# The low half of w_up's weights by an accumulating transfer: a decoder layer in split float32 on one core

## The chip, the core and the metric

The kernel runs on one core of a Trainium2 chip. The metric is the device time of one execution in microseconds (us). The kernel before takes 1471.77 us, the median of three runs (1471.39 to 1471.92).

## What is computed

One layer of a decoder over 256 tokens of 2048 channels, in float32: attention and a gated short convolution side by side, merged by gates and added to the residual r; then a wide MLP; then a gate with a per-layer input. The part that the change touches is the MLP, cut from the reference:

```python
D_MODEL = 2048
SEQ = 256
D_FF = 4 * D_MODEL
...
        r = r + merged @ w_o[i]
        h = rms_norm(r, g_mlp[i])
        r = r + jnp.square(jax.nn.relu(h @ w_up[i])) @ w_down[i]
        h = rms_norm(r, g_ple[i])
        r = r + jax.nn.sigmoid(h @ w_ple_gate[i]) * (p[i] @ w_ple_proj[i])
```

## The kernel before

TensorE multiplies in float32r, which keeps fewer bits than float32. So each operand is split into a high part (the value rounded to float32r) and a low part (value minus high), and each product is made of three: high by high, high by low, low by high. All weights come from HBM as float32 and are split on the core; activations are split when they are made.

A *unit* is 128x2048 weights, 1 MiB, loaded by one transfer that SP issues into one of three `raw` buffers. `load_unit` (L117) splits it in two halves of 128x1024: for each half ScalarE makes `w_hi` (L88) and VectorE `w_lo` (L89). The pool `wp` has 7 buffers of half a unit each for `hi` and for `lo`, so the half that is seventh after another takes its buffers, once TensorE has read them. `load_rows` (L128) does the same for w_down, in pieces of 128x512.

The MLP is a loop over q = 0 to 3. In each, 16 units of w_up give 16 sums `ps_up` (`cols` and `mm`, L168 to L184): per unit 16 blocks k, the first 8 in the first half and the others in the second, each with one matmul of the high weights on both parts of x (512 columns) and one of the low weights on the high part (256 columns). ScalarE and VectorE then take each sum out of its bank (L188, L189), apply relu and the row factor `row1` (L440), square it (L441) and split it (L88, L89). Then 16 units of w_down follow (L154 to L156, `ps_dn`).

`row1` comes from `rstd_mlp`: eight small matmuls after the first w_up unit (L207), a scaling on VectorE (L82), a power on GpSimd (L83), two diagonals on VectorE (L215), and a matmul after the second unit (L217).

Every engine runs its instructions in its own order, which the framework's scheduler sets from the order of the program and the buffers; semaphores hold an instruction until its inputs are there and its buffer is free.

Of the kernel before, what the change touches and what calls it, by code (L numbers as in the profile page):

```python
# [8 lines left out]
F32 = mybir.dt.float32  # L9
F32R = mybir.dt.float32r  # L10
AF = mybir.ActivationFunctionType
ALU = mybir.AluOpType
# [3 lines left out]
P = 128  # L16
# [8 lines left out]
HALF = UNIT // 2  # L25
# [10 lines left out]
def hybrid_block_kernel(ctx: ExitStack, tc: tile.TileContext, ins: dict, out: bass.AP):  # L36
# [9 lines left out]
    nc = tc.nc  # L46

    const = ctx.enter_context(tc.tile_pool(name="const", bufs=1))
    wp = ctx.enter_context(tc.tile_pool(name="wp", bufs=7))
# [5 lines left out]
    def slot(shape, dtype, name):  # L55
        return bp.tile(shape, dtype, tag="slot", name=name)

    def bank(name):
        return acc.tile([P, CW], F32, tag="acc", name=name)
# [25 lines left out]
    def split(hi, lo, src, gain=None):  # L85

        if gain is None:
            nc.scalar.activation(hi, src, AF.Copy)  # L88
            nc.vector.tensor_sub(lo, src, hi.bitcast(F32))  # L89
        else:  # L90
            nc.scalar.activation(hi, src, AF.Copy, scale=gain)
            nc.vector.scalar_tensor_tensor(lo, src, gain, hi.bitcast(F32), op0=ALU.mult, op1=ALU.subtract)

    def xsplit(xs, k, src, gain=None):

        x = slot([P, 2, S], F32R, "x")
        split(x[:, 0, :], x[:, 1, :], src, gain)
        xs[k] = x
# [4 lines left out]
    def run_pending(n):  # L103
        for _ in range(min(n, len(pending))):
            pending.pop(0)()


    def split_half(raw, step=HALF, between=None):
        hi = wp.tile([P, HALF], F32R, tag="hi", name="w_hi")
        lo = wp.tile([P, HALF], F32R, tag="lo", name="w_lo")  # L110
        for i in range(0, HALF, step):
            if between:
                between(i // step)
            split(hi[:, i:i + step], lo[:, i:i + step], raw[:, i:i + step])
        return hi, lo

    def load_unit(w):  # L117

        raw = wp.tile([P, UNIT], F32, tag="raw", name="raw", bufs=3)
        nc.sync.dma_start(raw, w)  # L120
        return [split_half(raw[:, h * HALF:(h + 1) * HALF]) for h in range(2)]

    def load_half(w):
        raw = wp.tile([P, HALF], F32, tag="raw", name="raw", bufs=3)
# [18 lines left out]
    def rows(units, xs, name, pops=1):  # L143

        nu = len(units)
        ps = [bank(f"ps_{name}_{t}") for t in range(NT)]
        for u, load in enumerate(units):
            wt = load()
            for j in range(KU):
                k = KU * u + j  # L150
                hi, lo = (p[:, (j % 2) * CW:(j % 2 + 1) * CW] for p in wt[j // 2])
                for t in range(NT):
                    xh, xl = (xs[k][:, i, t * P:(t + 1) * P] for i in range(2))
                    nc.tensor.matmul(ps[t], xh, hi, start=k == 0, stop=False)  # L154
                    nc.tensor.matmul(ps[t], xh, lo, start=False, stop=False)  # L155
                    nc.tensor.matmul(ps[t], xl, hi, start=False, stop=k == KU * nu - 1)  # L156
            run_pending(pops)
        return ps

    def qkv(c, load=load_unit):  # L160
        return [lambda u=u: load(ins["w_qkv"][c, u]) for u in range(4)]

    def tiles(wname, n, us=range(4)):

        w = ins[wname]
        return [lambda u=u: load_rows(w[n:n + 4, :, u * CW:(u + 1) * CW]) for u in us]

    def mm(ps, wt, i, x, first, last):  # L168

        wh, wl = (p[:, (i % 8) * P:(i % 8 + 1) * P] for p in wt[i // 8])  # L170
        both = x.rearrange("p a s -> p (a s)")
        if not last:
            nc.tensor.matmul(ps, wh, both, start=first, stop=False)  # L173
        nc.tensor.matmul(ps[:, S:], wl, x[:, 0, :], start=False, stop=False)  # L174
        if last:
            nc.tensor.matmul(ps, wh, both, start=False, stop=True)  # L176

    def cols(wt, xs, name, at=0, nk=16, flush=None):

        ps = bank(f"ps_{name}")  # L180
        for k in range(nk):
            if k == flush:
                run_pending(len(pending))
            mm(ps, wt, at + k, xs[k], k == 0, k == nk - 1)  # L184
        return ps

    def total(dst, ps):
        nc.scalar.activation(dst, ps[:, S:], AF.Copy)  # L188
        nc.vector.tensor_add(dst, ps[:, :S], dst)  # L189

    def temp(name):
        return sm.tile([P, S], F32, tag="temp", name=name, bufs=8)
# [10 lines left out]
    def rstd_columns(ss, name):  # L203
        ps = trp.tile([P, NT], F32, tag="tr", name=f"ps_ss_{name}")
        for t in range(NT):
            for i in range(2):
                nc.tensor.matmul(ps[:, t:t + 1], ss[:, i, t * P:(t + 1) * P], ones[:, 0:1], start=i == 0, stop=i == 1)  # L207
        rstd = const.tile([P, NT], F32, name=f"rstd_{name}")
        rsqrt_mean(rstd, ps, D, NT)
        return rstd  # L210

    def rstd_rows(rstd, name):
        diag = slot([P, NT, P], F32, f"diag_{name}")
        for t in range(NT):
            nc.vector.tensor_scalar_mul(diag[:, t, :], ident, rstd[:, t:t + 1])  # L215
        ps = trp.tile([P, S], F32, tag="tr", name=f"ps_rstd_{name}")
        nc.tensor.matmul(ps, ones, diag.rearrange("p t s -> p (t s)"), start=True, stop=True)  # L217
        row = const.tile([P, S], F32, name=f"rstd_row_{name}")
        nc.scalar.activation(row, ps, AF.Copy)
        return row  # L220
# [124 lines left out]
    for j in range(8):  # L345
        cc, cx, cb = temp("cc"), temp("cx"), temp("cb")
        for i, dst in ((1, cc), (2, cx), (0, cb)):
            total(dst, cols(load_unit(w_in[8 * i + j]), xT, f"conv{i}_{j}"))
            nc.vector.tensor_mul(dst, dst, row0)
            run_pending(1)  # L350
        u = sm.tile([P, S + 2], F32, tag="u", name=f"u_{j}")
        nc.gpsimd.memset(u[:, 0:2], 0.0)
        nc.vector.tensor_mul(u[:, 2:], cc, cx)
        y = temp("y")
        nc.scalar.activation(y, u[:, 2:], AF.Copy, scale=col(W_CONV + 16 + j))
        nc.vector.scalar_tensor_tensor(y, u[:, 1:S + 1], col(W_CONV + 8 + j), y, op0=ALU.mult, op1=ALU.add)
        nc.vector.scalar_tensor_tensor(y, u[:, 0:S], col(W_CONV + j), y, op0=ALU.mult, op1=ALU.add)
        nc.vector.tensor_mul(y, y, cb)
        xsplit(convT, j, y)


    def transposed(n, src, done):

        ps = trp.tile([P, 2, S], F32, tag="tr", name=f"tr_{n}")
        for i in range(2):
            o = (n + i) % 4 * P
            for t in range(NT):
                nc.tensor.transpose(ps[:, i, t * P:(t + 1) * P], src[t][:, o:o + P], ident)
        done(n, ps)
# [36 lines left out]
    hT = {}  # L406
    ss1 = slot([P, 2, S], F32, "ss1")
    for n in range(16):
        add_to_r(n, cols(load_unit(ins["w_o"][n]), mT, f"o_{n}", flush=12))
        xsplit(hT, n, r[n // 2][:, n % 2, :], col(G_MLP + n))  # L410
        if n % 2 == 1:
            square_sum(ss1, n // 2, r[n // 2])
# [14 lines left out]
    for q in range(4):  # L427
        uT = {}
        ready = []
        for n in range(16):  # L430
            ready.append(cols(load_unit(ins["w_up"][16 * q + n]), hT, f"up_{q}_{n}"))
            if q == 0 and n == 0:
                rstd1 = rstd_columns(ss1, "mlp")
                continue
            if q == 0 and n == 1:
                row1 = rstd_rows(rstd1, "mlp")
            for ps in ready:
                a = temp("a")
                total(a, ps)
                nc.vector.scalar_tensor_tensor(a, a, 0.0, row1, op0=ALU.max, op1=ALU.mult)  # L440
                nc.scalar.activation(a, a, AF.Square)  # L441
                xsplit(uT, len(uT), a)
            ready = []
        for c in range(4):
            ps = rows(tiles("w_down", 16 * q + 4 * c), uT, f"dn_{q}_{c}")
            for t in range(NT):
                if q == 0:
                    d[c, t] = slot([P, CW], F32, f"d_{c}_{t}")
                    nc.scalar.activation(d[c, t], ps[t], AF.Copy)
                else:  # L450
                    nc.vector.tensor_add(d[c, t], ps[t], d[c, t])
            if q == 3:
                for n in (4 * c, 4 * c + 2):
                    pending.append(lambda n=n, m=(d[c, 0], d[c, 1]): transposed(n, m, end_r))
# [23 lines left out]
    ready = []  # L478
    for n in range(16):
# [22 lines left out]
        ready = []  # L502
# [55 lines left out]
```

## Time and profile before

| what | value |
|---|---|
| median of three runs | 1471.77 us |
| the profiled execution's own time | 1472.05 us |
| its span, first to last instruction | 1470.1 us |
| TensorE matmul (PE) busy | 1459.7 us, 99% |
| VectorE (DVE) busy | 895.6 us, 61% |
| ScalarE (ACT) busy | 757.8 us, 52% |
| GpSimd (POOL) busy | 11.2 us, 1% |
| DMA engines, mean rate | 189 GB/s |

The span is the profiled execution between its first and last instruction; its own time also counts what lies around it. Busy times of engines overlap, so they don't add up to the span. In views of the trace, L12 is line 12 of the kernel, PEld is TensorE's weight load, SPq is the queue of transfers that SP issues.

### The profile page before, as it was taken

How to read it: one execution, taken by the hardware profiler on the slowest of the kernel's cores; microseconds unless marked ns; L12 is line 12 of the kernel's file. 1: busy time of each engine (PE TensorE's matmuls, PEld its weight loads, DVE VectorE, ACT ScalarE, POOL GpSimd, SP SyncE). 2: the span in 40 equal slices, each digit the busy share in tenths (PEclk: the TensorE clock that was granted, in tenths of full speed). 3: DMA queues.
4: the chain of work that ended last, by engine and by line, in shares of the span. 5: the costliest groups of instructions: out<-in, count | busy, mean ns of one | idle time of the engine just before them, and what ended most of it. 6: DMA issues, size and time to landing. Idle time of an engine off the chain costs nothing.

```text
span 1470.1 us, 18933 instructions
## 1 busy us (share of the span) xinstructions
PE 1459.7 (99%) x7384; PEld 1237.6 (84%) x7384; DVE 895.6 (61%) x1360; ACT 757.8 (52%) x1287; POOL 11.2 (1%) x27
## 2 busy tenths in 40 slices
PE   8999999999999999999999999999999999999998
PEld 6888888888888888888888888888888888888887
DVE  7555676756464547666654566555665466666775
ACT  7655555544445444445544455445554455545543
POOL 0100000000000000000000000000000000000000
PEclk9999999999999999999999999999999999999999
DMA  8644445555555565555555555555555555555551
GB/s 315 228 173 172 172 173 174 180 191 200 186 186 200 183 248 191 180 182 191 182 190 200 187 185 190 185 198 195 178 195 186 191 200 174 200 179 189 184 203 55
DMA packets 87305, 278.35 MB, mean 189 GB/s; under 512 B 5040, under 2 KB 7344, under 8 KB 69296
## 3 DMA queue, kind: packets, MB, share of 16 engines
q1 hardware_dynamic: 87072, 277.11, 54.5%
q8 instruction: 58, 0.95, 0.3%
q14 instruction: 31, 0.25, 0.0%
q10 hardware_dynamic: 144, 0.04, 0.0%
HBM read 275.03 MB, written 2.10 MB: 189 GB/s over the span
## 4 chain that ended last, share of the span: by engine, by line
PE 99%; DMA 0%; DVE 0%; ACT 0%; issue 0%
PE ps_up L173 15%; PE ps_up L174 8%; PE ps_dn L156 8%; PE ps_dn L154 8%; PE ps_dn L155 8%; PE ps_conv L173 6%; PE ps_g L156 4%; PE ps_g L154 4%; PE ps_g L155 4%; PE ps_o L173 4%; PE ps_pg L173 4%; PE ps_conv L174 3%; PE ps_o L174 2%; PE ps_pg L174 2%; PE ps_y L156 2%; PE ps_y L154 2%
## 5 line engine op out<-in xcount | busy, mean ns | idle before, releaser
L89 DVE TENSOR_TENSOR w_lo<-raw,w_hi 128x512 fp32r<-128x512 f32 (+1 forms) x748 | 647.8, 892 | 412.1 <-ACT w_hi L88 407.1
L88 ACT ACTIVATE w_hi<-raw 128x512 fp32r<-128x512 f32 (+1 forms) x748 | 568.6, 789 | 474.1 <-PE ps_dn L156 173.9
L173 PE MATMUL ps_up<-x,w_hi 128*128 128x512 f32 x960 | 341.7, 399 | 0.0
L174 PE MATMUL ps_up<-x,w_lo 128*128 128x256 f32 x1024 | 277.1, 281 | 0.0
L173 PEld LDWEIGHTS ps_up<-x,w_hi 128*128 128x128 f32 x960 | 180.4, 188 | 41.6
L154 PE MATMUL ps_dn<-w_hi,x 128*128 128x512 f32 x512 | 199.8, 390 | 0.0
L156 PE MATMUL ps_dn<-w_hi,x 128*128 128x512 f32 x512 | 199.3, 389 | 0.0
L155 PE MATMUL ps_dn<-w_lo,x 128*128 128x512 f32 x512 | 199.2, 389 | 0.0
L174 PEld LDWEIGHTS ps_up<-x,w_lo 128*128 128x128 f32 x1024 | 193.2, 189 | 6.3
L173 PE MATMUL ps_conv<-x,w_hi 128*128 128x512 f32 x360 | 129.5, 402 | 0.0
L156 PEld LDWEIGHTS ps_dn<-w_hi,x 128*128 128x128 f32 x512 | 96.1, 188 | 20.2
L155 PEld LDWEIGHTS ps_dn<-w_lo,x 128*128 128x128 f32 x512 | 96.1, 188 | 20.0
L154 PEld LDWEIGHTS ps_dn<-w_hi,x 128*128 128x128 f32 x512 | 96.1, 188 | 19.4
L174 PE MATMUL ps_conv<-x,w_lo 128*128 128x256 f32 x384 | 103.5, 280 | 0.0
L154 PE MATMUL ps_g<-w_hi,x 128*128 128x512 f32 x256 | 99.9, 390 | 0.0
L156 PE MATMUL ps_g<-w_hi,x 128*128 128x512 f32 x256 | 99.6, 389 | 0.0
L155 PE MATMUL ps_g<-w_lo,x 128*128 128x512 f32 x256 | 99.6, 389 | 0.0
L173 PE MATMUL ps_pg<-x,w_hi 128*128 128x512 f32 x240 | 85.8, 399 | 0.0
L188 ACT ACTIVATE a<-ps_up 128x256 f32<-128x256 f32 x64 | 24.6, 384 | 118.7 <-PE ps_up L176 118.7
L173 PE MATMUL ps_o<-x,w_hi 128*128 128x512 f32 x240 | 85.6, 399 | 0.0
L173 PEld LDWEIGHTS ps_conv<-x,w_hi 128*128 128x128 f32 x360 | 67.6, 188 | 15.2
L174 PEld LDWEIGHTS ps_conv<-x,w_lo 128*128 128x128 f32 x384 | 72.5, 189 | 1.4
(184 smaller groups left out, 1686.0 us busy)
## 6 DMA issues: line engine op xcount, KB each, us to landing
raw<-in_w_up_dram SPq DMA_DIRECT2D x64, 1024.0 KB, 4.9
raw<-in_w_down_dram SPq DMA_DIRECT2D x64, 1024.0 KB, 5.1
raw<-in_w_in_dram SPq DMA_DIRECT2D x56, 1024.0 KB, 5.0
raw<-in_w_qkv_dram SPq DMA_DIRECT2D x20, 1024.0 KB, 4.9
raw<-in_w_branch_dram SPq DMA_DIRECT2D x16, 1024.0 KB, 5.1
raw<-in_w_o_dram SPq DMA_DIRECT2D x16, 1024.0 KB, 4.9
raw<-in_w_ple_gate_dram SPq DMA_DIRECT2D x16, 1024.0 KB, 5.1
raw<-in_w_qkv_dram SPq DMA_DIRECT2D x16, 256.0 KB, 5.8
```

The source lines that it names most:

```text
L88: nc.scalar.activation(hi, src, AF.Copy)
L89: nc.vector.tensor_sub(lo, src, hi.bitcast(F32))
L154: nc.tensor.matmul(ps[t], xh, hi, start=k == 0, stop=False)
L155: nc.tensor.matmul(ps[t], xh, lo, start=False, stop=False)
L156: nc.tensor.matmul(ps[t], xl, hi, start=False, stop=k == KU * nu - 1)
L173: nc.tensor.matmul(ps, wh, both, start=first, stop=False)
L174: nc.tensor.matmul(ps[:, S:], wl, x[:, 0, :], start=False, stop=False)
L188: nc.scalar.activation(dst, ps[:, S:], AF.Copy)
```

## The change

In w_up alone, the second half of each unit is split in another way. ScalarE makes the high part as before, then writes minus high into the low buffer, and a transfer issued by GpSimd adds the raw half onto it in place. VectorE's subtraction of that half is gone. The first half, and all other weights, are split as before. There are 64 such halves (4 times 16).

```diff
+    def split_half_dma(raw):
+
+        hi = wp.tile([P, HALF], F32R, tag="hi", name="w_hi")
+        lo = wp.tile([P, HALF], F32R, tag="lo", name="w_lo")
+        nc.scalar.activation(hi, raw, AF.Copy)
+        nc.scalar.activation(lo, hi.bitcast(F32), AF.Copy, scale=-1.0)
+        nc.gpsimd.dma_start(lo, raw, accum_op=ALU.add)
+        return hi, lo
+
-    def load_unit(w):
+    def load_unit(w, by_dma=False):
 
         raw = wp.tile([P, UNIT], F32, tag="raw", name="raw", bufs=3)
         nc.sync.dma_start(raw, w)
-        return [split_half(raw[:, h * HALF:(h + 1) * HALF]) for h in range(2)]
+        return [(split_half_dma if by_dma and h else split_half)(raw[:, h * HALF:(h + 1) * HALF]) for h in range(2)]
...
-            ready.append(cols(load_unit(ins["w_up"][16 * q + n]), hT, f"up_{q}_{n}"))
+            ready.append(cols(load_unit(ins["w_up"][16 * q + n], by_dma=True), hT, f"up_{q}_{n}"))
```

The order of TensorE's and of SP's instructions is the same in both kernels (only line numbers differ, by 9 after the new function). On ScalarE, in the middle of the first w_up phase, one beat stands so before (the sum of unit 4 is taken out, and the weights of a unit further on are split):

```order
L188 ACTIVATE a_5701<-ps_up_0_4_5668 128x256
L88 ACTIVATE w_hi_5864<-raw_5862 128x1024
L441 ACTIVATE a_5701<-a_5701 128x256
L88 ACTIVATE x_5706<-a_5701 128x256
L88 ACTIVATE w_hi_5868<-raw_5862 128x1024
L188 ACTIVATE a_5752<-ps_up_0_5_5719 128x256
```

and so with the change:

```order
L197 ACTIVATE a_5706<-ps_up_0_4_5673 128x256
L88 ACTIVATE w_hi_5872<-raw_5870 128x1024
L450 ACTIVATE a_5706<-a_5706 128x256
L88 ACTIVATE x_5711<-a_5706 128x256
L121 ACTIVATE w_hi_5876<-raw_5870 128x1024
L122 ACTIVATE w_lo_5877<-w_hi_5876 128x1024
L197 ACTIVATE a_5758<-ps_up_0_5_5725 128x256
```

Minus high (L122) stands right behind the high part of the second half, ahead of the next sum's evacuation. On GpSimd, which had nothing to do between the convolution's memsets and the two powers, the queue now holds 64 transfers (L123), the first four of them ahead of the power for `rstd_mlp`:

```order
L361 MEMSET u_7_2620 128x2
L123 DMA w_lo_5446<-raw_5439 128x1024
L123 DMA w_lo_5498<-raw_5491 128x1024
L123 DMA w_lo_5565<-raw_5558 128x1024
L123 DMA w_lo_5617<-raw_5610 128x1024
L83 TENSOR_TENSOR rstd_mlp_5488<-rstd_mlp_5488,half_75 128x2
L123 DMA w_lo_5669<-raw_5662 128x1024
L123 DMA w_lo_5721<-raw_5714 128x1024
```

Before, the power followed directly on the last memset; now it can start only when the four transfers ahead of it have been issued.

## Rows read from the trace of the kernel before

**Rows 1.** The page: busy time, share of the span and instructions; engines' shares of the chain.

```profile
PE 1459.7 (99%) x7384; PEld 1237.6 (84%) x7384; DVE 895.6 (61%) x1360; ACT 757.8 (52%) x1287; POOL 11.2 (1%) x27
...
PE 99%; DMA 0%; DVE 0%; ACT 0%; issue 0%
```

**Rows 2.** What PE waited for, whole run: us in total, times, longest.

```profile
PE ps_q L154 <- ACT x L91: 5.6, 1, 5.6
```

**Rows 3.** Busy time by window: first w_up phase, w_down phase, last w_up phase.

```profile
core 0: us, PE busy (x) PEld busy (x) DVE busy (x) ACT busy (x) POOL busy (x), PEclk, DMA share, GB/s
647.00:737.00 90.00, 90.00 (x516) 78.33 (x515) 58.28 (x89) 51.58 (x86) 0.70 (x1) 1.00 0.54 187
737.00:825.00 88.00, 88.00 (x393) 72.94 (x392) 42.44 (x63) 40.79 (x68) 0.00 (x0) 1.00 0.56 191
...
1180.00:1271.00 91.00, 91.00 (x516) 78.87 (x515) 58.93 (x86) 50.88 (x83) 0.00 (x0) 1.00 0.53 185
```

**Rows 4.** The same view, three units of w_up one after another.

```profile
671.13:676.78 5.65, 5.65 (x33) 4.90 (x32) 3.64 (x5) 3.23 (x6) 0.00 (x0) 1.00 0.55 186
676.78:682.43 5.65, 5.65 (x33) 4.91 (x32) 3.63 (x5) 3.23 (x5) 0.00 (x0) 1.00 0.51 186
682.43:688.09 5.66, 5.66 (x33) 4.91 (x32) 3.63 (x5) 3.23 (x6) 0.00 (x0) 1.00 0.54 188
```

**Rows 5.** Timeline, ScalarE in one beat: start, us, instruction, idle before and releaser.

```profile
671.13 0.39 ACT L188 ACTIVATE a<-ps_up 128x256 f32<-128x256 f32 x1 [1.83 <-PE ps_up L176]
671.41 1.05 ACT L88 ACTIVATE w_hi<-raw 128x1024 fp32r<-128x1024 f32 x1
...
673.82 1.06 ACT L88 ACTIVATE w_hi<-raw 128x1024 fp32r<-128x1024 f32 x1 [0.49 <-PE ps_up L173]
...
676.78 0.38 ACT L188 ACTIVATE a<-ps_up 128x256 f32<-128x256 f32 x1 [1.90 <-PE ps_up L176]
```

**Rows 6.** Timeline, VectorE's low parts and SP's next load.

```profile
669.33 1.22 DVE L89 TENSOR_TENSOR w_lo<-raw,w_hi 128x1024 fp32r<-128x1024 f32 x1 [0.83 <-ACT w_hi L88]
670.58 11.57 SPq L120 DMA_DIRECT2D raw<-in_w_up_dram  x3
...
674.92 1.23 DVE L89 TENSOR_TENSOR w_lo<-raw,w_hi 128x1024 fp32r<-128x1024 f32 x1 [0.86 <-ACT w_hi L88]
```

**Rows 7.** What SP's queue waited for, whole run: us in total, times, longest.

```profile
SPq L120 <- DVE w_lo L89: 649.9, 130, 10.3
```

**Rows 8.** The page, transfers: count, KB each, median us from issue to landing.

```profile
raw<-in_w_up_dram SPq DMA_DIRECT2D x64, 1024.0 KB, 4.9
...
raw<-in_w_ple_proj_dram SPq DMA_DIRECT2D x4, 512.0 KB, 3.5
```

**Rows 9.** Groups by line and shape: count, busy us, mean ns of one, idle before.

```profile
L89 DVE TENSOR_TENSOR w_lo<-raw,w_hi 128x1024 fp32r<-128x1024 f32 x284 | 347.0, 1224 | 171.1 <-ACT w_hi L88 166.5
...
L88 ACT ACTIVATE w_hi<-raw 128x1024 fp32r<-128x1024 f32 x284 | 300.1, 1058 | 200.8 <-PE ps_dn L156 39.1 <-PE ps_up L173 30.0 <-PE ps_o L176 28.0
```

**Rows 10.** Line 120 in 670 to 700 us: ns min/median/max of one issue.

```profile
L120 SPq DMA_DIRECT2D raw<-in_w_up_dram x6: 328/328/328, 670.6 to 698.8; - x6
```

**Rows 11.** Timeline, the way to the row factor at the start of w_up.

```profile
650.18 1.06 ACT L88 ACTIVATE w_hi<-raw 128x1024 fp32r<-128x1024 f32 x1 [0.67 <-PE ps_up L173]
...
654.16 0.70 POOL L83 TENSOR_TENSOR rstd_mlp<-rstd_mlp,half 128x2 f32<-128x2 f32 x1 [393.02 <-DVE rstd_mlp L82]
654.90 0.48 DVE L215 TENSOR_SCALAR diag_mlp<-ident,rstd_mlp 128x128 f32<-128x128 f32 x2 [0.48 <-POOL rstd_mlp L83]
...
659.38 0.60 PE L217 MATMUL ps_rstd_mlp<-diag_mlp,ones 128*128 128x256 f32 x2
```

**Rows 12.** The page, DMA queues: packets, MB, share of 16 engines.

```profile
q1 hardware_dynamic: 87072, 277.11, 54.5%
```

**Rows 13.** DMA in 671 to 682.3 us, 40 slices: busy tenths, GB/s.

```profile
DMA  0693847999899400000009814999999871000000
GB/s 0 87 232 58 174 174 290 464 464 406 348 435 406 174 0 0 0 0 0 0 0 116 145 29 174 377 406 406 435 464 406 377 319 58 0 0 0 0 0 0
```

## Prediction

> **What bounds the kernel now.** I first read the page's busy times and its chain: TensorE is busy for 1459.7 us of a span of 1470.1 us, and the chain that ended last is 99% TensorE [rows 1]. A busy PE could still hide waits, so I next asked for what PE waited for: one entry in the whole run, 5.6 us at the first matmul [rows 2]. Then the stages that the change touches: in the first and the last w_up phase and in the w_down phase between, PE is busy for the full length of the window, at a granted clock of 1.00, the upper level of 2.4 GHz [rows 3]. So inside w_up nothing can be gained by making VectorE shorter; VectorE's work there lies wholly beside matmuls. The question is only whether the new path stays as well hidden as the old one was. What the reader needs for that is the beat of one unit: three successive units of w_up take 5.65, 5.65 and 5.66 us, with ScalarE busy for 3.23 and VectorE for 3.63 us of each [rows 4].
>
> **How far ahead the weights are.** Seven hi and seven lo buffers of half a unit mean that half h+7 goes into the buffers of half h. The cycle is plain on ScalarE [rows 5]: TensorE ends a unit just before 671.13; ScalarE makes the high part of the first half of the unit four ahead at 671.41 and of its second half at 673.82, each when TensorE lets a buffer go. TensorE comes to that unit three beats after 671.1, at 688.1, and to its second half at 690.9. The low part that VectorE makes at 674.92 to 676.15 [rows 6] is thus 14.8 us early.
>
> The raw buffers are the tighter ring. There are three, and SP issues the next load as soon as VectorE's second half is done: 669.33 + 1.22 = 670.55, load at 670.58 [rows 6]; SP waits for just this 130 times, 649.9 us in all [rows 7]. A load lands in 4.9 us [rows 8], so a buffer freed at 676.15 is full at 681.05, and is wanted at 671.41 + 16.96 = 688.4: 7.3 us to spare.
>
> **The change, part by part.**
>
> *Removed from VectorE:* 64 subtractions of 128x1024 at 1224 ns [rows 9] = 78.3 us. All of it lay beside full TensorE windows [rows 3]: gain 0.
>
> *Added on ScalarE:* 64 activations of 128x1024, which I take at the 1058 ns of the same shape [rows 9] = 67.7 us. The high part ends at 674.88; minus high would run to 675.94; the next thing ScalarE must do is to evacuate the sums at 676.78, before which it sits idle for 1.90 us [rows 5]. It fits with 0.8 us over, and its load goes from 3.23 to 4.29 us of 5.65. Price 0. If that cover were gone, the evacuation would be late by some tenths of a us, and nobody on TensorE waits for it before the banks come round.
>
> *The subtraction becomes a transfer.* Call L the time from the end of minus high (675.94) to the landing of the sum. Two limits follow. For TensorE: 690.9 - 675.94 = 15.0 us. For the raw ring, as the transfer reads raw: 675.94 + L + 4.9 must not pass 688.4, so L plus the load's time may be 12.4 us, which is L up to 7.5 us beside a 4.9 us load. Past that, the ring of three runs late by a third of the excess per unit.
>
> The trace has no accumulating transfer and none issued by GpSimd, so L is bounded. Nearest rows: a 512 KB load lands in 3.5 us and a 1024 KB one in 4.9 us, both with their fixed part [rows 8]. One pass over 512 KB is 3.5; an addition that reads two operands moves 1024 KB on the reading side, 4.9; a third pass for the write would make it 6.3, by the same step of 1.4. Issue: SP needs 328 ns a load [rows 10], GpSimd's only work here takes 0.70 us [rows 11]; I take 0.7, with 0.3 and 1.4 as bounds. Sharing: the queue is busy for 54.5% of the span to move 277.11 MB [rows 12], so 801 us of all 16 engines, 3.03 us for each 1 MiB unit; a transfer that runs beside a load waits for between none and all of that. Low end: 3.5 + 0.3 = 3.8 us. High end: 6.3 + 1.4 + 3.0 = 10.7 us. I take two reads, half of a load in the way: 4.9 + 0.7 + 1.5 = 7.1 us, because the operation names two inputs and the load it meets is busy for about half of the beat. That is under 7.5 us, if not by much: price 0. Nothing excludes the values above it, so they go into the range.
>
> Engine time must fit as well: 5.65 - 3.03 = 2.62 us of all 16 engines is free per unit. One pass of 512 KB takes half of 3.03 = 1.5 us; two take 3.0 at the mean rate, or 1.05 MB / 464 GB/s = 2.3 us at the best slices of a w_up window [rows 13]. So two reads are on the edge, not clearly inside.
>
> Here a rule bears on the change. The Trainium skill (Collectives: The Full Stack, "The bandwidth ceiling: the fold count and why AG ≠ RS ≠ AR") says that an addition in the transfer costs no time of its own, but has two source reads on one read ring, so that it moves half as fast as a copy. No run shows that yet. By it the engine time would be the 3.0 us just given, 0.4 over what is free, and the result that of the late ring below; by the best slices it would be the forecast.
>
> *Queues.* SP's next load now waits for the transfer instead of VectorE; behind it stand only further loads of the same ring, which the limit above covers. On GpSimd the one operation that meets the transfers is the power for rstd_mlp, which now stands behind four transfers. The fourth belongs to the half whose high part ran at 650.18 to 651.24; minus high would end at about 652.3 and its issue at about 653.0 to 653.7, while the power started at 654.16 [rows 11]. Even if it slips, TensorE takes the product only at 659.38, and VectorE had its factor ready at 655.38 [rows 11]: 4.0 us of cover. Price 0.
>
> **The sum.** VectorE 0, ScalarE 0, transfers 0, queues 0: the profiled execution took 1472.05 us (span 1470.1, 1.95 around it), and stays there. It lies 0.28 us above the median of 1471.77, so I say 1471.8, own range 1470.3 to 1473.5. I call under 0.2%, 2.9 us, no change.
>
> **The rivals.**
>
> *Slower: the raw ring turns late.* If transfer and load share the engines throughout, both stretch. Take L = 4.9 + 0.7 + 2.7 = 8.3 and the load 4.9 + 1.5 = 6.4: 14.7 against 12.4, 2.3 too much, 0.77 us per unit, 12.3 us in a phase of 16 units. TensorE feels it when the lead of 15.0 - 8.3 = 6.7 us is used up: 5.6 us a phase, 22 us in four, 1494 us. The high end, L = 10.7 beside an unstretched load, gives 16 x 3.2 / 3 = 17.1 less 4.3 = 12.8, four times is 51: 1523 us. It decides from L plus load = 12.4 us, and is felt only from L = 8.7, where 16/3 of the excess over 7.5 has used up the lead of 15.0 - L. For it: the engines are already 54 to 56% busy in these windows [rows 3]; against it: peak slices reach 464 GB/s [rows 13], and the w_down phases refill the lead.
>
> *Much slower: the addition is no stream.* If an engine does read, add and write one after another without overlap, it holds the engines for far longer than 3 us. Each us over 2.62 then costs 64 units x 1 us, less the lead of four phases, 4 x 6.7 = 27 us: 5 us per transfer would be 64 x 2.4 - 27, some 125 us, 1597 us; 8 us, some 317 us, 1789 us. For it: no row shows the operation at all, so no rate is proven. Against it: nothing in the trace; it is merely not seen.
>
> *Faster.* VectorE's 78 us could pay only where TensorE waits for VectorE; there is no such wait [rows 2], and the 10.4 us in which TensorE is idle lie outside w_up.
>
> *The change does not do what it says*, that is, the transfers finish as early as VectorE did and nothing waits longer: this is the forecast's time.
>
> **How the numbers follow.** Forecast (hidden, including the last case) 0.50; ring late 0.29; no stream 0.19; faster 0.02. So faster 0.02, within 0.2% 0.50, slower 0.48. The range goes from 1469.5 to 1560: below, the spread of the runs; above, the whole of the late ring and the mildest of the last kind (L near 12, 16 x 4.5 / 3 - 3 = 21 a phase, 84 us), which leaves out about 0.16.
>
> **What would show it.** Right: PE's waits still list only the start, the w_up windows stay 5.65 us a unit, the transfers land within 7.5 us, the queue's share rises from 0.54 to about 0.8 or more in w_up. Ring late: SP waits for the transfers, ScalarE's high parts wait for loads, then PE ps_up waits for w_lo or w_hi, late in each phase rather than early. No stream: PE waits from the fourth unit of every phase and the engines are full. ScalarE up by 68 us and VectorE down by 78 us must show in every case. A gain of over 3 us, or a loss that lies at rstd_mlp, would prove the reading of the bound wrong.

## The result and the profile after

The changed kernel takes 1479.84 us, the median of three runs (1476.9 to 1487.06), against 1471.77 us before: a ratio of 1.0065, 95% interval 1.0048 to 1.0083. That is 8 us slower, inside the range given. It is not the forecast's "no change" but the mild end of the first rival, the late ring of raw buffers. The runs also lie wider apart than before, 10 us against 0.5.

The profiled execution took 1479.84 us with a span of 1478.0 us. Its page: busy times, the two DMA queues (q0 is the new one, issued by GpSimd), and the issues of w_up's loads and of the new transfers (median us to landing).

```profile
PE 1461.1 (99%) x7384; PEld 1237.8 (84%) x7384; DVE 816.8 (55%) x1296; ACT 813.1 (55%) x1351; POOL 65.8 (4%) x91
...
q1 hardware_dynamic: 87072, 277.11, 54.3%
q0 software_dynamic: 9216, 33.56, 12.1%
...
raw<-in_w_up_dram SPq DMA_DIRECT2D x64, 1024.0 KB, 6.6
...
w_lo<-raw POOLq DMA_DIRECT2D x64, 512.0 KB, 7.3
```

Against [rows 1], VectorE is down by 78.8 us, as worked out (78.3). ScalarE is up by 55.3 us and not by 68, although the 64 new activations do take 67.9 us:

```profile
L122 ACT ACTIVATE w_lo<-w_hi 128x1024 fp32r<-128x1024 f32 x64 | 67.9, 1060 | 2.0
```

In the trace the records of activations that follow each other at once overlap by some 0.1 us (in the rows of e8 below, 692.99 + 0.42 against 693.31), and the page counts such time once. TensorE's idle time went from 1470.1 - 1459.7 = 10.4 us to 1478.0 - 1461.1 = 16.9 us, 6.5 us more, and its busy time up by 1.4: together the 7.9 us of the span. A load of w_up now lands in 6.6 us, against 4.9 in [rows 8].

What TensorE waited for (total us, times, longest), to set beside the single entry of [rows 2]:

```profile
PE ps_up L183 <- DMA w_lo<-raw: 6.4, 7, 1.7
PE ps_q L163 <- ACT x L91: 5.5, 1, 5.5
```

The whole new idle time is seven waits for the new transfer. Busy time by window, the four phases of w_up, and behind the first three their w_down:

```profile
core 0: us, PE busy (x) PEld busy (x) DVE busy (x) ACT busy (x) POOL busy (x), PEclk, DMA share, GB/s
647.00:737.00 90.00, 89.00 (x507) 76.93 (x505) 37.36 (x66) 58.03 (x89) 12.04 (x15) 1.00 0.92 246
737.00:825.00 88.00, 86.56 (x386) 71.71 (x386) 43.78 (x70) 46.05 (x79) 1.70 (x2) 1.00 0.64 216
825.00:915.00 90.00, 89.72 (x504) 77.47 (x503) 34.94 (x59) 59.13 (x88) 11.87 (x14) 1.00 0.95 256
915.00:1003.00 88.00, 87.77 (x394) 72.66 (x393) 48.16 (x77) 43.91 (x75) 1.70 (x2) 1.00 0.63 214
1003.00:1092.00 89.00, 88.76 (x498) 76.67 (x497) 34.04 (x56) 56.26 (x81) 11.87 (x14) 1.00 0.93 252
1092.00:1180.00 88.00, 86.33 (x388) 71.47 (x388) 50.50 (x81) 44.09 (x78) 0.84 (x1) 1.00 0.67 219
1180.00:1271.00 91.00, 89.33 (x498) 77.01 (x497) 35.02 (x57) 59.18 (x86) 12.76 (x15) 1.00 0.92 245
```

Subtracting busy from length, phase by phase, TensorE loses 2.4, 0.5, 1.9 and 1.7 us. The windows are those of [rows 3] and slide a little against the phases, so the losses that show in a w_down window are of the last units of w_up. The DMA share of the w_up windows rose from 0.54 to between 0.92 and 0.95, as the prediction's "about 0.8 or more" says.

The chain that leads to those waits starts with ScalarE, whose high parts now wait for loads of w_up; in [rows 5] they wait for TensorE. And in w_up SP's next load now waits for the new transfer, where it waited for VectorE [rows 7]. Waits of ScalarE, then of SP's queue:

```profile
ACT w_hi L88 <- DMA raw<-in_w_up_dram: 97.1, 44, 5.4
```

```profile
SPq L129 <- DMA w_lo<-raw: 327.9, 52, 10.1
```

So a raw buffer goes round: load, split, transfer, load. From 651 us to the end of the first phase, while this ring sets the pace, both of its transfers are longer than their medians over the whole run:

```profile
raw<-in_w_up_dram SPq DMA_DIRECT2D x11, 1024.0 KB, 7.3
w_lo<-raw POOLq DMA_DIRECT2D x13, 512.0 KB, 7.6
```

The pace of that ring is seen in GpSimd's issues, here the first of 14 in a row in the first phase, two in the middle and the last:

```profile
646.38 0.85 POOL L123 DMA_DIRECT2D w_lo<-raw  x1 [4.77 <-ACT w_lo L122]
...
684.64 0.84 POOL L123 DMA_DIRECT2D w_lo<-raw  x1 [8.12 <-ACT a L197]
689.63 0.86 POOL L123 DMA_DIRECT2D w_lo<-raw  x1 [4.14 <-ACT a L197]
...
731.01 0.85 POOL L123 DMA_DIRECT2D w_lo<-raw  x1 [7.09 <-ACT a L197]
```

13 intervals in 84.63 us are 6.51 us a unit, where TensorE wants one every 5.65. In the kernel before, the high parts of the same two second halves start at:

```profile
644.53 1.06 ACT L88 ACTIVATE w_hi<-raw 128x1024 fp32r<-128x1024 f32 x1 [1.24 <-PE ps_o L173]
...
719.05 1.06 ACT L88 ACTIVATE w_hi<-raw 128x1024 fp32r<-128x1024 f32 x1 [0.49 <-PE ps_up L173]
```

That is 74.52 us for the same 13 intervals, so the change falls 10.1 us behind in this phase. TensorE had a lead to spend first, which is why it lost only about 2.4 us in the phase.

### The profile page after: what moved, and what is told of

Same layout as the page of the kernel before. It is cut to its first block, busy times and chain, and to the rows that moved or that the text cites. A ratio compares the mean times of both kernels' runs of the same rounds, so it can differ in the third digit from the quotient of the medians.

```text
span 1478.0 us, 19190 instructions
## 1 busy us (share of the span) xinstructions
PE 1461.1 (99%) x7384; PEld 1237.8 (84%) x7384; DVE 816.8 (55%) x1296; ACT 813.1 (55%) x1351; POOL 65.8 (4%) x91
## 3 DMA queue, kind: packets, MB, share of 16 engines
q0 software_dynamic: 9216, 33.56, 12.1%
## 5 line engine op out<-in xcount | busy, mean ns | idle before, releaser
L89 DVE TENSOR_TENSOR w_lo<-raw,w_hi 128x512 fp32r<-128x512 f32 (+1 forms) x684 | 568.7, 861 | 465.7 <-ACT w_hi L88 462.8
L88 ACT ACTIVATE w_hi<-raw 128x512 fp32r<-128x512 f32 (+1 forms) x684 | 499.9, 763 | 511.8 <-PE ps_dn L165 128.0
L123 POOL DMA_DIRECT2D w_lo<-raw x64 | 54.6, 853 | 953.0 <-ACT w_lo L122 728.6
L121 ACT ACTIVATE w_hi<-raw 128x1024 fp32r<-128x1024 f32 x64 | 67.2, 1050 | 25.0 <-PE ps_dn L165 14.9
L182 PEld LDWEIGHTS ps_conv<-x,w_hi 128*128 128x128 f32 x360 | 67.7, 188 | 15.2
```

The lines of the kernel that those rows point to most:

```text
L121: nc.scalar.activation(hi, raw, AF.Copy)
L123: nc.gpsimd.dma_start(lo, raw, accum_op=ALU.add)
```

## The experiments

All runs are compared with the kernel before on the same chip. Theories: the **ring** (a raw buffer is held until the transfer has landed, and transfer plus load take longer than the ring allows); the **engines** (the 16 DMA engines are simply full in w_up); ScalarE's added work; a fixed cost of the path by GpSimd.

**The change again (e1).** No edit.

> The changed kernel itself, once more, beside the others on the same chip. Every theory: slower than before by 5 to 15 us, with some us of spread from run to run, and PE waiting for w_lo by the transfer late in the w_up phases.

Measured: 1479.21 us, ratio 1.0053 (1.0034 to 1.0071), ten runs from 1473.26 to 1486.2. The execution that was profiled is the fastest of the ten:

```profile
raw<-in_w_up_dram SPq DMA_DIRECT2D x64, 1024.0 KB, 6.4
...
w_lo<-raw POOLq DMA_DIRECT2D x64, 512.0 KB, 6.8
```

Load and transfer together take 13.2 us here, 13.9 us in the execution above that lost 8. Both are over the 12.4 us of the prediction; here the lead covers nearly all of what the ring falls behind, and TensorE waits for the new transfer once, for 0.7 us. This suggests a kernel on the edge, where some tenths of a us per transfer become several us; two executions don't prove it.

**Without the transfer (e2).**

```diff
-        nc.gpsimd.dma_start(lo, raw, accum_op=ALU.add)
```

> The transfer is left out, minus high stays in the low buffer; all else is as in the changed kernel. This leaves ScalarE's added 68 us and VectorE's lost 78 us alone. Ring theory (raw buffers are held until the transfer lands, and load plus transfer exceed 12.4 us) and engine theory (the 16 DMA engines are full in w_up): 1471.8 us within 1 us, PE waits only at the start. If ScalarE's added work were the cause: about 1480 us as with the transfer.

Measured: 1472.16 us, 1.0001 (0.9992 to 1.0011). ScalarE's 64 activations and VectorE's missing 64 subtractions are worth nothing either way; the price of 0 for both holds.

**A copy instead of an addition (e3).**

```diff
-        nc.gpsimd.dma_start(lo, raw, accum_op=ALU.add)
+        nc.gpsimd.dma_start(lo, raw)
```

> The transfer copies raw over minus high instead of adding, so the low part is raw itself: same issue, same waits, one operand read instead of two. Both ring and engine theory: engine time of a transfer falls from 2.8 to about 1.5 us, landing from 7.3 to about 5 us, the raw load lands in 5 to 5.5 us, and the loss is gone (1471.8 within 1.5 us). If the loss came from the path by GpSimd as such (its issue, its semaphores), 1478 to 1482 us would stay.

Measured: 1471.49 us, 0.9999 (0.9990 to 1.0008). The page's queue, the loads and the transfers:

```profile
q0 software_dynamic: 9216, 33.56, 6.5%
...
raw<-in_w_up_dram SPq DMA_DIRECT2D x64, 1024.0 KB, 5.5
...
w_lo<-raw POOLq DMA_DIRECT2D x64, 512.0 KB, 4.9
```

The same bytes on the same path and the same order of waits, and no loss, so the path by GpSimd costs nothing as such. The raw buffer is held here too, but load and transfer take 10.4 us together. Engine time: 6.5% of 1470.1 us over 64 transfers is 1.49 us each; with the addition, 12.1% of 1478.0 is 2.79 us. The addition costs the engines 1.87 times a copy. For the adding step of a collective, the Trainium skill (Collectives: The Full Stack, "The bandwidth ceiling: the fold count and why AG ≠ RS ≠ AR") explains half the speed of a copy by two source reads. Carried over to this transfer that would be a factor of 2; the 1.87 measured here nearly agrees.

**The first half instead of the second (e4).**

```diff
-        return [(split_half_dma if by_dma and h else split_half)(raw[:, h * HALF:(h + 1) * HALF]) for h in range(2)]
+        return [(split_half_dma if by_dma and not h else split_half)(raw[:, h * HALF:(h + 1) * HALF]) for h in range(2)]
```

> The first half of each unit goes by the transfer, the second by VectorE: the same 64 transfers, but each starts some 2.4 us earlier in the life of its raw buffer, so the buffer is freed about 2.4 us earlier. Ring theory: load plus transfer may now be about 14.8 us, against 13.9 measured, so the loss falls below 2 us (1471.8 to 1473.8). Engine theory: the engines carry the same work, so the loss stays at 5 to 10 us (1477 to 1482).

Measured: 1471.77 us, 1.0001 (0.9992 to 1.0010). This is the run that parts the theories. Same transfers, same bytes, same result of the layer; in the second and the last w_up phase:

```profile
825.00:915.00 90.00, 90.00 (x510) 78.01 (x510) 41.20 (x70) 60.46 (x98) 11.06 (x13) 1.00 0.99 275
...
1180.00:1271.00 91.00, 91.00 (x515) 78.86 (x514) 44.15 (x73) 60.30 (x96) 11.09 (x13) 1.00 0.99 277
```

The engines are fuller than with the change (0.99 against 0.92 to 0.95), and move more (275 to 277 GB/s against 245 to 256), yet TensorE is busy throughout these windows, so full engines by themselves cost nothing. The wait for the transfer is still there, nearly as long as the 327.9 us with the change:

```profile
SPq L129 <- DMA w_lo<-raw: 295.8, 52, 9.6
```

What is gone is a piece of the ring: the transfer now runs while ScalarE and VectorE split the second half, so a buffer goes round sooner.

**Raw freed before the transfer (e5).**

```diff
-        nc.scalar.activation(lo, hi.bitcast(F32), AF.Copy, scale=-1.0)
-        nc.gpsimd.dma_start(lo, raw, accum_op=ALU.add)
+        nc.scalar.activation(lo, raw, AF.Copy)
+        nc.gpsimd.dma_start(lo, hi.bitcast(F32), accum_op=ALU.add)
```

> ScalarE copies raw into the low buffer and the transfer adds the high half onto it (the low part is then raw plus high instead of raw minus high): the same transfer, the same engines, the same wait of TensorE, but raw is no longer read by it and is freed by ScalarE at about 676 us of the beat shown. Ring theory: no loss (1471.8 within 1.5 us), and SP no longer waits for a transfer. If TensorE's own wait for a late landing, or full engines, were the cause: 1476 to 1482 us as with the change.

Measured: 1471.61 us, 0.9999 (0.9990 to 1.0009). The page's issues, and the window of the second w_up phase:

```profile
raw<-in_w_up_dram SPq DMA_DIRECT2D x64, 1024.0 KB, 9.3
...
w_lo<-w_hi POOLq DMA_DIRECT2D x64, 512.0 KB, 10.1
```

```profile
825.00:915.00 90.00, 90.00 (x510) 77.98 (x509) 40.51 (x70) 64.53 (x99) 11.90 (x14) 1.00 1.01 278
```

SP's loads of w_up now wait for ScalarE, and no longer for a transfer:

```profile
SPq L129 <- ACT w_lo L122: 88.9, 42, 2.4
```

Loads and transfers are both far slower than with the change, 9.3 and 10.1 us, because only the split holds a load back and both queues run at once; the engines are full. And nothing is lost. Even these transfers stay inside TensorE's own limit (15.0 us), and full engines do no harm here. What is left as the cause is the transfer's hold on the raw buffer.

**Four raw buffers (e6).** All four places that take a raw buffer get `bufs=4`, of which one is shown. To make room, the small temporaries get 5 buffers.

```diff
-        raw = wp.tile([P, UNIT], F32, tag="raw", name="raw", bufs=3)
+        raw = wp.tile([P, UNIT], F32, tag="raw", name="raw", bufs=4)
...
-        return sm.tile([P, S], F32, tag="temp", name=name, bufs=8)
+        return sm.tile([P, S], F32, tag="temp", name=name, bufs=5)
```

> The change with four raw buffers instead of three (and 5 buffers instead of 8 for the small temporaries, to make room). Ring theory: the limit for load plus transfer rises by one beat, from 12.4 to 18.0 us, so the loss is gone: 1471.8 to 1473.5 us, unless the temporaries cost something elsewhere. Engine theory: the loss stays near 1479.

Measured: 1471.37 us, 0.9998 (0.9988 to 1.0007). A transfer lands in 7.4 us and a load in 6.3 us, nearly as with the change (7.3 and 6.6), and the loss is gone. That is the ring shown from its other side.

**Both halves (e7).**

```diff
-        return [(split_half_dma if by_dma and h else split_half)(raw[:, h * HALF:(h + 1) * HALF]) for h in range(2)]
+        return [(split_half_dma if by_dma else split_half)(raw[:, h * HALF:(h + 1) * HALF]) for h in range(2)]
```

> Both halves of each unit by the transfer, 128 in all. Engine time per unit is then 3.0 for the load and 2 x 2.8 for the transfers, 8.6 us against a beat of 5.65: here the engines must bind whatever the ring does. 16 x 2.95 less a lead of about 8 to 10 us is 37 to 39 us a phase, about 150 us in four: 1610 to 1640 us. If instead the measured shares of engine time do not add up (transfers and loads overlap on an engine), much less: 1490 to 1560 us.

Measured: 1582.78 us, 1.0752 (1.0736 to 1.0768): 111 us lost, less than the 150 expected. The queue, and in the first phase GpSimd's issue for the first half of one unit and of the tenth after it:

```profile
q0 software_dynamic: 18432, 67.12, 22.2%
```

```profile
662.86 0.88 POOL L123 DMA_DIRECT2D w_lo<-raw  x1 [6.84 <-ACT w_lo L122]
...
743.07 0.84 POOL L123 DMA_DIRECT2D w_lo<-raw  x1 [5.96 <-ACT x L88]
```

80.21 us over 10 units are 8.02 us a unit, where the sum of engine times said 8.6. Over 64 units the missing 0.6 us are 37 us, which nearly closes the gap of 39. The engine time of a transfer was nearly right (22.2% of 1582.0 us over 128 transfers is 2.74 us). The times don't simply add: the DMA share of the window reads 1.03, so 8.02 us hold about 8.3 us of engine time. SP waits for transfers here as well, 52 times, so this run alone doesn't part the ring from the engines; but 8.3 us of engine time can't go into a beat of 5.65.

```profile
647.00:737.00 90.00, 76.59 (x409) 64.32 (x407) 15.55 (x39) 54.56 (x78) 19.35 (x23) 0.96 1.03 259
```

**Six buffers for the halves (e8), and the same on the kernel before (e9).**

```diff
-    wp = ctx.enter_context(tc.tile_pool(name="wp", bufs=7))
+    wp = ctx.enter_context(tc.tile_pool(name="wp", bufs=6))
```

> The change with six instead of seven buffers for high and for low halves: the lead is 2.83 us shorter in each phase, the ring of raw is as it was. Ring theory: lateness of the ring is the same and TensorE feels more of it, up to 2.83 us more in each of four phases: 1483 to 1491 us. If the lead plays no part: about 1479, as with the change.

> The kernel before with six instead of seven buffers for high and for low halves, no transfer added: the control for the run of the change with six. Every theory: the lead of 14.8 us falls to about 12 us and is still not used up, 1471.8 us within 1.5 us. If it is slower by itself, that part is taken off what the change with six buffers showed.

Measured: e9 1472.12 us, 1.0003 (0.9993 to 1.0012), so the buffer costs nothing by itself. e8 1500.65 us, 1.0197 (1.0175 to 1.0219): 29 us lost where 11 to 19 were expected. The lead counts, but it was not the only thing that moved. ScalarE in the middle of the first phase of e8:

```profile
689.85 1.06 ACT L88 ACTIVATE w_hi<-raw 128x1024 fp32r<-128x1024 f32 x1 [4.80 <-DMA raw<-in_w_up_dram]
...
691.08 1.05 ACT L121 ACTIVATE w_hi<-raw 128x1024 fp32r<-128x1024 f32 x1
692.99 0.42 ACT L450 ACTIVATE a<-a 128x256 f32<-128x256 f32 x1 [0.87 <-DVE a L449]
693.31 1.04 ACT L122 ACTIVATE w_lo<-w_hi 128x1024 fp32r<-128x1024 f32 x1
```

The same place in a beat of the change, with seven buffers:

```profile
680.49 1.06 ACT L88 ACTIVATE w_hi<-raw 128x1024 fp32r<-128x1024 f32 x1 [3.93 <-DMA raw<-in_w_up_dram]
...
683.29 1.06 ACT L122 ACTIVATE w_lo<-w_hi 128x1024 fp32r<-128x1024 f32 x1
```

With six buffers the scheduler puts the squaring (L450) between the second half's high part and minus high, and it waits there for VectorE. From the first half's high part to minus high it is 693.31 - 689.85 = 3.46 us, against 683.29 - 680.49 = 2.80 us with seven, where the squaring runs before the second half's high part. So each transfer starts about 0.7 us later in the ring. As an estimate, a third of that over 13 intervals is 3 us a phase, 12 in four, and the shorter lead gives up to 2.83 us a phase, 11 in four: 23 us, beside the some 21 us that e8 loses more than the change, a part of which is a lower granted clock (last section). No run separates the shares.

**Every second unit (e10).**

```diff
-            ready.append(cols(load_unit(ins["w_up"][16 * q + n], by_dma=True), hT, f"up_{q}_{n}"))
+            ready.append(cols(load_unit(ins["w_up"][16 * q + n], by_dma=n % 2 == 1), hT, f"up_{q}_{n}"))
```

> The transfer in every second unit of w_up only, 32 in all. Ring theory: of the three raw buffers in turn at most two are held late, and loads meet half as many transfers, so load plus transfer averages well under 12.4 us with the lead to spare: 1471.8 us within 1.5 us, not half of the loss. If each transfer cost a fixed amount on the path: half of the loss, about 1475.5 us.

Measured: 1471.67 us, 1.0000 (0.9991 to 1.0009). Half of the transfers cost not half of the loss but none of it; loads land in 5.0 us and transfers in 4.5:

```profile
raw<-in_w_up_dram SPq DMA_DIRECT2D x64, 1024.0 KB, 5.0
...
w_lo<-raw POOLq DMA_DIRECT2D x32, 512.0 KB, 4.5
```

## Why the prediction was right in its range and wrong in its likeliest case

**The bound** was read rightly: nothing is gained from VectorE's 78.8 us, and nothing was lost by ScalarE's 67.9 us (e2). The path by GpSimd costs nothing as such (e3; and e4 to e6 keep the addition's longer issue and lose nothing), and the power for rstd_mlp started at 653.57 us in the changed kernel, before the 654.16 of [rows 11].

**The length of the transfer** was nearly right: 7.1 us forecast; measured are 0.3 us from minus high to the issue and 7.3 us to landing, 7.6 together. So was its engine time, 3.0 us by the mean rate against 2.79.

**The limits** were right in kind. TensorE's 15.0 us never counted by itself (e5). The ring's limit for transfer plus load did: moving the transfer earlier in the life of the buffer (e4), freeing the buffer (e5) or adding one (e6) each removes the whole loss. Its 12.4 us were somewhat strict. In the late ring ScalarE starts as a load lands and is through with minus high 684.35 - 680.49 = 3.9 us later, where the prediction had 4.5, so the limit is about 16.96 - 3.9 = 13.0 us.

**The step that failed** is "L up to 7.5 us beside a 4.9 us load". The shared engines were charged to the transfer, 1.5 us of its 7.1, while the load beside it was left at the 4.9 us of [rows 8], which is the time of a load with the engines to itself. Both pay. The load went to 6.6 us, 1.7 more, and the transfer was 0.5 longer than forecast, so the sum was 0.3 + 7.3 + 6.6 = 14.2 us against 12.4. With 1.5 us charged to the load too, the prediction's own numbers give 7.1 + 6.4 = 13.5: a ring that turns late, but by 1.1 / 3 x 16 = 5.9 us a phase, still less than the lead of 15.0 - 7.1 = 7.9. It took both terms: with 14.2 the same sum gives 9.6 us a phase against a lead of 7.4, so 2.2 lost, 8.8 in four, where 8.1 were measured. That it comes so near is partly luck: the 14.2 are medians over units that wait and units that don't, while the ring in its stride had 0.3 + 7.6 + 7.3 = 15.2 us against 13.0, so 0.73 us a unit for 13 intervals and not 16: 9.5 us, near the 10.1 seen in the first phase. The late ring with its 8.3 + 6.4 = 14.7 had this right, and was called the less likely.

**The size of that rival** was too large: 22 us against 8. It charged 12.3 us of lateness a phase; the first phase falls 10.1 us behind, and the lead is about 15.0 - 7.6 = 7.4 us and not 6.7, so 2.7 us should show; TensorE lost 2.4 there. In the other phases the same 13 intervals take 81.37, 80.86 and 82.06 us, against 73.25 before: the ring falls only 8.1, 7.6 and 8.8 us behind, barely more than the lead, and TensorE lost 0.5, 1.9 and 1.7. Single transfers land in 4.5 to 10.5 us, so a lead by the median doesn't give each phase exactly. Why the later phases run less late is not settled; so near the limit small changes in when loads and transfers meet decide, which is also the likeliest reading of the wide spread of the runs (1473 to 1486 us in e1). That reading is argued from two executions, not shown by a run of its own.

**The engines** were feared for the wrong reason. Sharing them is what stretches both lengths, but their being full costs nothing by itself. The "5.65 - 3.03 = 2.62 us" of free time and the 2.79 used are nearly equal, and the share did rise to 0.95; but the fuller engines of e4 and e5 lose nothing. They must decide where their time clearly exceeds the beat (e7). "No stream" is out: the addition takes 1.87 times the engine time of a copy, as two operands would, and not "far longer than 3 us".

## What to carry to other kernels

When work moves from an engine to a transfer, look at what the transfer *holds*: here it kept an input buffer for about 8.7 us after the high part was made (1.1 for minus high, then 7.6), where VectorE had kept it for 676.15 - 674.88 = 1.3, and the ring of loads behind it turned too slowly, while the consumer itself had time to spare. Where a transfer must read a buffer of a short ring, put it on the part that is ready first, or let it read something else. And when two transfers share the engines, stretch both of them in the sum, not only the new one.

## What the runs showed that was not expected

GpSimd needs longer to issue the addition than the copy: 853 ns against 534 ns each, in the changed kernel and in e3.

```profile
L123 POOL DMA_DIRECT2D w_lo<-raw x64 | 54.6, 853 | 953.0 <-ACT w_lo L122 728.6 <-ACT a L197 209.3 <-DVE a L198 9.3
```

```profile
L123 POOL DMA_DIRECT2D w_lo<-raw x64 | 34.2, 534 | 957.4 <-ACT w_lo L122 926.7 <-ACT a L197 24.7 <-ACT x L88 6.0
```

And where TensorE had waited, its matmuls could run slower. In e8 it waited 2.8 us at the end of the first phase, and the granted clock of that stretch is 0.83, a mean of the levels of 1.2 and 2.4 GHz, against 1.00 in the stretch before, where it was never idle:

```profile
640.00:720.00 80.00, 80.00 (x457) 69.48 (x457) 32.01 (x56) 50.08 (x75) 11.82 (x14) 1.00 0.90 246
720.00:740.00 20.00, 17.19 (x82) 14.56 (x82) 8.41 (x15) 11.07 (x19) 1.70 (x2) 0.83 0.89 229
```

In e8 the matmuls were busy for 1468.7 us and in e7 for 1488.6, with the same instructions that take 1459.7 us before, so these two losses are not all waiting. In the profiled execution of the changed kernel the granted clock stayed at 1.00 in every window above, so there it plays no part. Its run of 1487.06 us has a mean granted clock of 0.997; no trace of it was kept.
